# Attention scores of a hybrid encoder block: 64-row plus 128-row products become two 128-row products

## The chip, the core and the metric

The kernel runs on one core of one Trainium2 chip. The metric is device time in microseconds (us) of one execution. The core's engines work side by side and meet through semaphores: TensorE (PE, with its weight loads listed apart as PEld), VectorE (DVE), ScalarE (ACT), GpSimd (POOL), and SyncE (SP), which here issues every DMA of the program, in order.

## The reference

A block over 2048 tokens of width 1024 has two mixers side by side, an RWKV-7 group and a differential-attention group, then an output projection, a residual, and a gated feed-forward layer with a short convolution. The part that matters here is the scores of the attention group: 4 heads, each with two maps (m = 0, 1) of head dimension 64.

```python
q = _rms_norm(q.reshape(bsz, T, B_HEADS, 2, B_HEAD_DIM), q_norm_w)
k = _rms_norm(k.reshape(bsz, T, B_HEADS, 2, B_HEAD_DIM), k_norm_w)
...
s = jnp.einsum('bhmqd,bhmkd->bhmqk', q_blk, k_t).astype(jnp.float32) * scale
s = jnp.where(allowed, s + bias, -jnp.inf)
p = jax.nn.softmax(s, axis=-1)
attn = p[:, :, 0] - lam * p[:, :, 1]
```

## The kernel before

Every large product is made of parts: a float32 operand is split into a high part, `hi`, that TensorE's format holds, and the rest, `lo`; a product is then hi·hi + hi·lo + lo·hi, summed in PSUM. For most products (lines 211 to 213, 243 to 245, 960 to 962, 1003 to 1005) that is three matmuls of 128 rows.

The scores have only 64 rows (the head dimension) per map. In DRAM the queries of a head lie as three slabs of 128 rows (`g.qd`, line 1024) and the keys as two (`g.kd`). With q and k split into hi and lo, slab 0 of the queries is [lo of map 0; hi of map 0], slab 1 is [hi of map 1; lo of map 1], slab 2 is [hi of map 0; hi of map 1]. The keys' slab 0 is [hi; lo] of map 0, slab 1 is [lo; hi] of map 1. So a score tile takes two matmuls: line 719 multiplies the 64 rows of hi by hi (rows 0 to 63 of the array for map 0, 64 to 127 for map 1), and line 720 multiplies 128 rows, lo·hi + hi·lo at once.

The program runs in stages. First the input projections with the RWKV units among them (to about 1060 us of the profiled execution); then the last projections (lines 243 to 245) with the first nine steps of attention among them; then the feed-forward layer of the first half of the tokens with the rest of attention among it (to about 2390 us); at the end the feed-forward layer of the second half alone. `finish_qk` (line 264) makes the parts of queries and keys, in tiles of the tag "x" (4 buffers, shared with `vs` of `proj_v`), and stores them. `Attention.heads` steps over blocks of 256 queries and heads; each step runs `scores` of one block and head and `values` of the one before. `scores` loads the queries of the block into `qs` (line 702, two buffers), then runs over two tiles of 128 queries, two maps, and chunks of up to 512 keys; line 723 takes each score tile out of PSUM on VectorE. No table sets the order of instructions: a scheduler that simulates the engines orders the program as a whole, and each engine then keeps its order.

Of the kernel before, what the change touches and what calls it, by code (L numbers as in the profile page):

```python
# [9 lines left out]
F32 = mybir.dt.float32  # L10
F32R = mybir.dt.float32r
# [8 lines left out]
P = 128  # L20
D = 1024
KT = D // P
T = 2048
# [29 lines left out]
NH = 4  # L53
# [3 lines left out]
QB = 256  # L57
# [39 lines left out]
def split_ps(g, ps, hi, lo, scale=None):  # L97

    nc = g.nc
    if scale is None:  # L100
        nc.scalar.copy(hi, ps)
        nc.vector.tensor_sub(lo, ps, hi.bitcast(F32))
    else:
        nc.scalar.activation(hi, ps, AF.Identity, scale=scale)
        nc.vector.scalar_tensor_tensor(lo, ps, scale, hi.bitcast(F32), ALU.mult, ALU.subtract)  # L105
# [34 lines left out]
def phase1(g, ctx):  # L140
    nc, tc, a = g.nc, g.tc, g.a
    rctx = ExitStack()
    cp = rctx.enter_context(tc.tile_pool(name="p1c", bufs=1, side="right"))
    sp = rctx.enter_context(tc.tile_pool(name="p1", bufs=1, side="right"))
# [104 lines left out]
    def proj_qk(tb, hT, gi):  # L249

        qz = dn.tile([P, 4, 256], F32, name="qz", tag="qz", bufs=QZB)
        ss = dn.tile([P, 4, 4], F32, name="qss", tag="qss")
        for j, ps in token_major(tb, hT, gi):
            r1 = rsa[:, 4 * tb + j:4 * tb + j + 1]
            nc.scalar.activation(qz[:, j, :], ps, AF.Identity, scale=r1)
            sq = dn.tile([P, 256], F32, name="qsq", tag="qsq", bufs=1)
            for i in range(4):
                d = slice(i * 64, i * 64 + 64)
                nc.scalar.activation(sq[:, d], qz[:, j, d], AF.Square, accum_out=ss[:, j, i:i + 1])
        rs = dn.tile([P, 16], F32, name="qrs", tag="qrs", bufs=2)  # L260
        rsqrt(g, dn, rs, ss.rearrange("p j g -> p (j g)"), 1.0 / 64, EPS, 16, "q")
        return lambda: finish_qk(tb, gi, qz, rs)

    def finish_qk(tb, gi, qz, rs):
        is_q = gi < 9
        q3 = qz.rearrange("p j (g d) -> p (j g) d", d=64)
        nc.gpsimd.tensor_mul(q3, q3, rs.unsqueeze(2).broadcast_to((P, 16, 64)))
        for hl_ in range(2):
            h = (gi - 7) % 2 * 2 + hl_
            ps = ps_mm.tile([P, TB], F32, name="tp", tag="mm")  # L270
            for j in range(4):
                nc.tensor.transpose(ps[:, j * P:(j + 1) * P], qz[:, j, hl_ * P:(hl_ + 1) * P], ident)
            hi = dn.tile([P, TB], F32R, name="qhi", tag="x", bufs=XB)
            lo = dn.tile([P, TB], F32R, name="qlo", tag="x", bufs=XB)
            split_ps(g, ps, hi, lo, qws[:, h:h + 1] if is_q else v("kw"))
            tsl = slice(tb * TB, (tb + 1) * TB)
            dd = (g.qd if is_q else g.kd)[h].rearrange("s p t -> (s p) t")[:, tsl]
            own = dd[0:256].rearrange("(m p) t -> m p t", p=64)[0::3]
            mid = dd[64:192]
            for dst, src in ((mid, hi), (own, lo), (dd[256:384], hi)) if is_q else ((own, hi), (mid, lo)):  # L280
                nc.sync.dma_start(out=dst, in_=src.bitcast(F32))

    def proj_v(tb, hT, gi):
# [56 lines left out]
    ps = ps_mm.tile([P, 2], F32, name="lam", tag="mm")  # L340
# [312 lines left out]
class Attention:  # L653
# [44 lines left out]

    def scores(self, i, h, kg, s0s):
        g, sp, nc = self.g, self.sp, self.g.nc  # L700
        qs = sp.tile([P, 3, QB], F32R, name="qs", tag="qs", bufs=2)
        nc.sync.dma_start(out=qs.bitcast(F32), in_=g.qd[h, :, :, i * QB:(i + 1) * QB].rearrange("s p t -> p s t"))
        es = []
        for qt in range(2):
            nk = i * QB + (qt + 1) * P
            q0 = i * QB + qt * P
            nch = (nk + 511) // 512
            qsl = slice(qt * P, (qt + 1) * P)
            parts = [slice(c0, min(nk, c0 + EW)) for c0 in range(0, nk, EW)]
            ss = sp.tile([P, 2, len(parts)], F32, name="ssum", tag="ssum", bufs=2)  # L710
            e = []
            for m in range(2):
                z = [sp.tile([P, EW], F32, name=f"e{m}", tag=f"e{m}", bufs=self.eb if m == 0 else self.e1b) for _ in parts]
                mx = sp.tile([P, 4], F32, name="mx", tag="mx", bufs=2)
                for ci in range(nch):
                    n = min(512, nk - ci * 512)
                    ps = self.ps_sc.tile([P, 512], F32, name="sc", tag="sc")
                    hr = slice(0, 64) if m == 0 else slice(64, 128)
                    nc.tensor.matmul(ps[:, 0:n], qs[hr, 2, qsl], kg[ci][hr, m, 0:n], start=True, stop=False)  # L719
                    nc.tensor.matmul(ps[:, 0:n], qs[:, m, qsl], kg[ci][:, m, 0:n], start=False, stop=True)  # L720
                    b0 = (T - P) - q0 + ci * 512
                    z0 = ci * 512 % EW
                    nc.vector.tensor_tensor_reduce(z[ci * 512 // EW][:, z0:z0 + n], ps[:, 0:n], self.nd[:, b0:b0 + n], 1.0,  # L723
                                                   -3e38, ALU.add, ALU.max, mx[:, ci:ci + 1])
                nm = sp.tile([P, 1], F32, name="nm", tag="nm", bufs=2)
                nc.vector.tensor_reduce(out=nm, in_=mx[:, 0:nch], axis=AX.X, op=ALU.max)
                nc.vector.tensor_scalar(nm, nm, -SLOPES[h], None, ALU.mult)  # L727
                for pi, p in enumerate(parts):
                    zp = z[pi][:, 0:p.stop - p.start]
                    nc.scalar.activation(zp, zp, AF.Exp, bias=nm, scale=SLOPES[h], accum_out=ss[:, m, pi:pi + 1])  # L730
                e.append(z)
            st = ss[:, :, 0]
            if len(parts) == 2:
                st = sp.tile([P, 2], F32, name="ssum2", tag="ssum2", bufs=2)
                nc.vector.tensor_add(st, ss[:, :, 0], ss[:, :, 1])
            cc = sp.tile([P, 1], F32, name="cc", tag="cc", bufs=2)
            nc.vector.reciprocal(cc, st[:, 1:2])
            nc.vector.tensor_mul(cc, cc, st[:, 0:1])
            nc.vector.tensor_mul(cc, cc, g.nlam)
            for c0 in range(0, nk, 512):  # L740
                e0, e1 = [x[c0 // EW][:, c0 % EW:c0 % EW + min(512, nk - c0)] for x in e]
                nc.vector.scalar_tensor_tensor(e0, e1, cc, e0, ALU.mult, ALU.add)
            nc.vector.tensor_copy(s0s[:, qt, h:h + 1], st[:, 0:1])
            es.append(e[0])
        return es
# [268 lines left out]
def build(tc, aps, ntb=T // TB, phases=(1, 2, 3), taps=None):  # L1014
    g = Ctx()
    g.nc, g.tc, g.a, g.ntb = tc.nc, tc, aps, ntb
    taps = taps or {}
    with ExitStack() as ctx:
        dp = ctx.enter_context(tc.tile_pool(name="scratch", bufs=1, space=DRAM))

        def scratch(n, shape):
            return taps[n] if n in taps else dp.tile(shape, F32, name=n)

        g.qd = scratch("qd", [NH, 3, P, T])
        g.kd = scratch("kd", [NH, 2, P, T])
        g.vd = scratch("vd", [T, 2, B_W])
        g.yd = scratch("yd", [T, A_W])
# [104 lines left out]
```

## Time and profile before

| | |
|---|---|
| median of 3 runs | 3371.3 us (3357.81 to 3382.51) |
| profiled execution | 3374.99 us, of it 3373.2 us span |
| PE busy | 3271.8 us (97%), mean granted clock 0.962 |
| DVE, ACT, POOL busy | 61%, 45%, 20% of the span |
| DMA | 557.42 MB, mean 165 GB/s |

A busy PE is not yet PE at its peak: a matmul's duration in the trace reaches over the start of the next, since matmuls are pipelined. What a matmul takes in a stream is read from one start to the next. A clock of 1.00 in a stretch is the full 2.4 GHz, and 0.5 the lower level, 1.2 GHz.

### The profile page before, as it was taken

Reading aid. Unit: us, or ns where it says so; the run is one execution under the profiler, and the core shown is the slowest. Engines: PE = TensorE matmul, PEld = TensorE weight load, DVE = VectorE, ACT = ScalarE, POOL = GpSimd, SP = SyncE. Lnnn points to the kernel's source line nnn. Section 1 sums busy time; section 2 is a strip of 40 time slices with the busy share of each in tenths; the row PEclk is TensorE's granted clock in tenths of the full one; section 3 lists DMA queues with packets and bytes.
Section 4 is the critical chain, followed back from the end, with each engine's and each line's share of the span. In section 5 each row is a group of like instructions: output and inputs, shape, how many; then the busy total and the mean of one; then the engine's idle time right before and its main releaser. Section 6 shows DMA issues by size and latency. Waiting matters only on the chain.

```text
span 3373.2 us, 54070 instructions
## 1 busy us (share of the span) xinstructions
PE 3271.8 (97%) x19314; PEld 2687.4 (80%) x19314; DVE 2073.9 (61%) x5939; ACT 1524.8 (45%) x3391; POOL 659.9 (20%) x501
## 2 busy tenths in 40 slices
PE   8999999999999899899999999999999999999999
PEld 6777778878888788788777777777888888888887
DVE  4888868788863555677667676666643444444444
ACT  5666555555654564444444454444433322222221
POOL 4112122341322012254443101011110000000010
PEclk9999989888999899899999999999999999999999
DMA  8765544344464767455655645554574323222322
GB/s 296 252 200 176 166 144 132 108 131 145 138 193 155 251 210 256 129 199 178 208 176 195 229 153 171 176 188 155 190 281 168 100 88 113 93 83 96 104 94 94
DMA packets 391453, 557.42 MB, mean 165 GB/s; under 512 B 81040, under 2 KB 204176, under 8 KB 391056
## 3 DMA queue, kind: packets, MB, share of 16 engines
q1 hardware_dynamic: 391184, 553.96, 50.9%
q8 instruction: 153, 2.51, 0.3%
q14 instruction: 116, 0.95, 0.1%
HBM read 436.39 MB, written 117.44 MB: 164 GB/s over the span
## 4 chain that ended last, share of the span: by engine, by line
PE 85%; DMA 7%; DVE 5%; ACT 1%; issue 1%; SPq 0%; POOL 0%; ACTq 0%; DVEq 0%; POOLq 0%
PE up L962 10%; PE up L960 10%; PE up L961 10%; PE dn L1003 5%; PE dn L1004 5%; PE dn L1005 5%; PE sc L720 3%; PE sc L719 3%; PE mm L243 2%; PE mm L212 2%; PE mm L211 2%; PE mm L213 2%; PE mm L244 2%; PE mm L245 2%; PE y L569 2%; PE y L567 2%
## 5 line engine op out<-in xcount | busy, mean ns | idle before, releaser
L961 PE MATMUL up<-hT,fwhi 128*128 128x512 f32 (+1 forms) x1536 | 580.1, 379 | 0.0
L960 PE MATMUL up<-hT,fwhi 128*128 128x512 f32 (+1 forms) x1536 | 573.9, 377 | 0.9 <-DVE halo L969 0.9
L962 PE MATMUL up<-hT,fwlo 128*128 128x512 f32 (+1 forms) x1536 | 569.5, 377 | 4.5 <-DMA fwlo<-lo_w_ffn_up 4.5
L967 DVE SCALAR_TENSOR_TENSOR yy<-up,vec,yy 128x511 f32<-128x511 f32 x352 | 262.1, 745 | 349.3 <-ACT yy L964 349.1
L1006 DVE TENSOR_TENSOR acc<-dn,acc 128x512 f32<-128x512 f32 x352 | 236.7, 688 | 188.0 <-PE dn L1005 187.3
L962 PEld LDWEIGHTS up<-hT,fwlo 128*128 128x128 f32 x1536 | 291.3, 190 | 59.1 <-DMA fwlo<-lo_w_ffn_up 7.0
L961 PEld LDWEIGHTS up<-hT,fwhi 128*128 128x128 f32 x1536 | 291.2, 190 | 51.4
L960 PEld LDWEIGHTS up<-hT,fwhi 128*128 128x128 f32 x1536 | 290.0, 190 | 52.3 <-DVE halo L969 1.2
L723 DVE CUSTOM_DVE_ANT_0 e<-sc,nd 128x512 f32<-128x512 f32 (+3 forms) x320 | 191.4, 608 | 202.5 <-PE sc L720 159.8
L990 POOL TENSOR_TENSOR gl<-yy,gh 128x512 fp32r<-128x512 f32 (+1 forms) x64 | 105.8, 1654 | 1015.7 <-ACT gh L989 844.0
L117 ACT CAST fwhi<-fwraw 128x1024 fp32r<-128x1024 f32 x164 | 172.1, 1049 | 284.1 <-PE up L961 189.2
L1004 PE MATMUL dn<-dlo,gh 128*128 128x512 f32 x704 | 275.6, 392 | 1.0 <-DMA dlo<-lo_w_ffn_down 1.0
L964 ACT ACTIVATE yy<-up,vec 128x512 f32<-128x512 f32 x176 | 136.4, 776 | 305.6 <-PE up L962 305.3
L1003 PE MATMUL dn<-dhi,gh 128*128 128x512 f32 x704 | 273.7, 397 | 0.2 <-ACT dhi L117 0.2
L1005 PE MATMUL dn<-dhi,gl 128*128 128x512 f32 x704 | 261.0, 392 | 0.0
L243 PE MATMUL mm<-whi,hh 128*128 128x256 f32 x768 | 239.7, 314 | 13.7 <-DVE vs L105 8.6
L244 PE MATMUL mm<-wlo,hh 128*128 128x256 f32 x768 | 234.9, 307 | 1.5 <-DMA wlo<-lo_w_in_b 1.5
L245 PE MATMUL mm<-whi,hl 128*128 128x256 f32 x768 | 230.4, 305 | 0.0
L730 ACT ACTIVATE e<-e,nm 128x1024 f32<-128x1024 f32 (+4 forms) x192 | 171.6, 896 | 72.1 <-DVE nm L727 69.3
L211 PE MATMUL mm<-hh,whi 128*128 128x512 f32 x448 | 187.4, 420 | 10.0 <-ACT hh L201 6.8
L117 ACT CAST whi<-wraw 128x512 fp32r<-128x512 f32 x208 | 127.7, 618 | 144.2 <-PE mm L212 61.9
L212 PE MATMUL mm<-hl,whi 128*128 128x512 f32 x448 | 187.5, 418 | 0.5 <-DVE hl L202 0.5
(278 smaller groups left out, 7406.3 us busy)
## 6 DMA issues: line engine op xcount, KB each, us to landing
fwraw<-in_w_ffn_up_dram SPq DMA_DIRECT2D x132, 512.0 KB
fwlo<-lo_w_ffn_up SPq DMA_DIRECT2D x88, 512.0 KB
draw<-in_w_ffn_down_dram SPq DMA_DIRECT2D x132, 256.0 KB
vg<-vd SPq DMA_DIRECT2D x128, 256.0 KB
wraw<-in_w_in_a_dram SPq DMA_DIRECT2D x112, 256.0 KB
wraw<-in_w_in_b_dram SPq DMA_DIRECT2D x96, 256.0 KB
lo_w_ffn_up<-fwlo SPq DMA_DIRECT2D x44, 512.0 KB
dlo<-lo_w_ffn_down SPq DMA_DIRECT2D x88, 256.0 KB
```

What stands on the lines that cost most here:

```text
L117: nc.scalar.copy(hi, raw)
L212: nc.tensor.matmul(ps, whi[k], hl[k], start=False, stop=False)
L243: nc.tensor.matmul(ps, hh[k][:, ts_], whi[k], start=k == 0, stop=False)
L244: nc.tensor.matmul(ps, hh[k][:, ts_], wlo[k], start=False, stop=False)
L245: nc.tensor.matmul(ps, hl[k][:, ts_], whi[k], start=False, stop=k == KT - 1)
L960: nc.tensor.matmul(ps[:, q], wh[:, k % 4, cs], xh, start=k == 0, stop=False)
L961: nc.tensor.matmul(ps[:, q], wh[:, k % 4, cs], xl, start=False, stop=False)
L962: nc.tensor.matmul(ps[:, q], wl[:, k % 4, cs], xh, start=False, stop=k == KT - 1)
L967: nc.vector.scalar_tensor_tensor(yn[:, d:], ps[:, 0:512 - d], w, yn[:, d:], ALU.mult, ALU.add)
L1003: nc.tensor.matmul(ps, gh_[:, tsl], dh_, start=gi == 0, stop=False)
L1004: nc.tensor.matmul(ps, gh_[:, tsl], dl_, start=False, stop=False)
L1005: nc.tensor.matmul(ps, gl_[:, tsl], dh_, start=False, stop=gi == FG - 1)
```

## The change

The queries are kept as two slabs, slab 0 hi of both maps and slab 1 lo of both maps, each stored once: two stores of a head and 512 tokens instead of three. `scores` allocates one tile per map with two slabs, [hi; hi] and [lo; lo]: each is loaded by two DMAs, the same 64 rows of DRAM into the upper and into the lower half of the rows. That is four DMAs of 128 KB for a block and head instead of one of 384 KB. The tiles are two thirds as large, with three buffers instead of two. The two matmuls of a score tile now both have 128 rows: hi·(hi + lo) and lo·(hi + lo); the sum also takes in lo·lo, which was left out before.

```diff
@@ finish_qk
-            dd = (g.qd if is_q else g.kd)[h].rearrange("s p t -> (s p) t")[:, tsl]
-            own = dd[0:256].rearrange("(m p) t -> m p t", p=64)[0::3]
-            mid = dd[64:192]
-            for dst, src in ((mid, hi), (own, lo), (dd[256:384], hi)) if is_q else ((own, hi), (mid, lo)):
+            if is_q:
+                pieces = ((g.qd[h, 0, :, tsl], hi), (g.qd[h, 1, :, tsl], lo))
+            else:
+                dd = g.kd[h].rearrange("s p t -> (s p) t")[:, tsl]
+                pieces = ((dd.rearrange("(m p) t -> m p t", p=64)[0::3], hi), (dd[64:192], lo))
+            for dst, src in pieces:
                 nc.sync.dma_start(out=dst, in_=src.bitcast(F32))
@@ scores
-        qs = sp.tile([P, 3, QB], F32R, name="qs", tag="qs", bufs=2)
-        nc.sync.dma_start(out=qs.bitcast(F32), in_=g.qd[h, :, :, i * QB:(i + 1) * QB].rearrange("s p t -> p s t"))
+        qs = []
+        for m in range(2):
+            q2 = sp.tile([P, 2, QB], F32R, name="qs", tag="qs", bufs=3)
+            src = g.qd[h, :, m * 64:m * 64 + 64, i * QB:(i + 1) * QB].rearrange("s p t -> p s t")
+            for hf in range(2):
+                nc.sync.dma_start(out=q2[hf * 64:hf * 64 + 64].bitcast(F32), in_=src)
+            qs.append(q2)
...
-                    hr = slice(0, 64) if m == 0 else slice(64, 128)
-                    nc.tensor.matmul(ps[:, 0:n], qs[hr, 2, qsl], kg[ci][hr, m, 0:n], start=True, stop=False)
-                    nc.tensor.matmul(ps[:, 0:n], qs[:, m, qsl], kg[ci][:, m, 0:n], start=False, stop=True)
+                    nc.tensor.matmul(ps[:, 0:n], qs[m][:, 0, qsl], kg[ci][:, m, 0:n], start=True, stop=False)
+                    nc.tensor.matmul(ps[:, 0:n], qs[m][:, 1, qsl], kg[ci][:, m, 0:n], start=False, stop=True)
@@ build
-        g.qd = scratch("qd", [NH, 3, P, T])
+        g.qd = scratch("qd", [NH, 2, P, T])
```

The order of the program also moves. In the rows below a row is line, operation, what is written, what is read, and the size; the number behind a name tells apart the tiles that were made under that name.

The first place is TensorE in a late step of attention, among the feed-forward layer's matmuls. Before:

```order
L771 MATMUL at_22599<-ident_83,e0_21920 128x128
L719 MATMUL sc_22713<-kg_22699,qs_22707 128x512
L720 MATMUL sc_22713<-kg_22699,qs_22707 128x512
L771 MATMUL at_22599<-ident_83,e0_21980 128x128 x2
L961 MATMUL up_25723<-hT10_24419,fwhi_25718 128x512
L962 MATMUL up_25723<-hT00_24418,fwlo_25719 128x512
L719 MATMUL sc_22717<-kg_22701,qs_22707 128x512
L720 MATMUL sc_22717<-kg_22701,qs_22707 128x512
```

The same place now, where lines 725, 726, 777, 967 and 968 are the former 719, 720, 771, 961 and 962:

```order
L777 MATMUL at_22695<-ident_83,e0_22012 128x128
L725 MATMUL sc_22813<-kg_22795,qs_22803 128x512
L726 MATMUL sc_22813<-kg_22795,qs_22803 128x512
L777 MATMUL at_22695<-ident_83,e0_22072 128x128 x2
L967 MATMUL up_25835<-hT10_24527,fwhi_25830 128x512
L968 MATMUL up_25835<-hT00_24526,fwlo_25831 128x512
L725 MATMUL sc_22817<-kg_22797,qs_22803 128x512
L726 MATMUL sc_22817<-kg_22797,qs_22803 128x512
```

Here nothing moved: pairs of score products stand between the same matmuls as before.

The second place is SyncE's queue where attention begins; `kg` are keys, `vg` values, `qs` queries. Before:

```order
L694 DMA kg_12745<-kd_58 128x2x512
L702 DMA qs_12749<-qd_57 128x3x256
L702 DMA qs_12994<-qd_57 128x3x256
L757 DMA vg_13050<-vd_59 128x2x128 x2
L694 DMA kg_13263<-kd_58 128x2x512
L757 DMA vg_13321<-vd_59 128x4x128 x2
```

Now, with line 708 for the former 702:

```order
L708 DMA qs_12741<-qd_57 64x2x256 x2
L708 DMA qs_12744<-qd_57 64x2x256 x2
L708 DMA qs_12990<-qd_57 64x2x256 x2
L763 DMA vg_13050<-vd_59 128x2x128 x2
L696 DMA kg_13263<-kd_58 128x2x512
L763 DMA vg_13325<-vd_59 128x4x128 x2
L696 DMA kg_13802<-kd_58 128x2x512
L696 DMA kg_14343<-kd_58 128x2x512
L290 DMA vd_59<-vs_13709 256x1x256
L290 DMA vd_59<-vs_13719 256x1x256
L290 DMA vd_59<-vs_13765 256x1x256
L708 DMA qs_12993<-qd_57 64x2x256 x2
```

Before, the queries of the first two steps (12749, 12994) were both loaded at once. Now the first step has two tiles (12741, 12744), the second step's map 0 (12990) takes the third buffer, and its map 1 (12993) follows with eight rows between, where the first step gives a buffer back.

The third place is TensorE in the second of these steps. Before:

```order
L720 MATMUL sc_12791<-kg_12745,qs_12749 128x256
L719 MATMUL sc_12999<-kg_12745,qs_12994 128x384
L720 MATMUL sc_12999<-kg_12745,qs_12994 128x384
L719 MATMUL sc_13009<-kg_12745,qs_12994 128x384
L720 MATMUL sc_13009<-kg_12745,qs_12994 128x384
L719 MATMUL sc_13026<-kg_12745,qs_12994 128x512
```

Now, with line 813 for the former 807:

```order
L813 MATMUL ott_13072<-ident_83,ot_13070 128x128 x2
L243 MATMUL mm_13932<-whi_13909,hh0_12525 128x256
L244 MATMUL mm_13932<-wlo_13910,hh0_12525 128x256
L245 MATMUL mm_13932<-whi_13909,hl0_12533 128x256
L243 MATMUL mm_13932<-whi_13909,hh1_12526 128x256
L244 MATMUL mm_13932<-wlo_13910,hh1_12526 128x256
L245 MATMUL mm_13932<-whi_13909,hl1_12534 128x256
L243 MATMUL mm_13932<-whi_13915,hh2_12527 128x256
L725 MATMUL sc_13009<-kg_12737,qs_12993 128x384
L726 MATMUL sc_13009<-kg_12737,qs_12993 128x384
L725 MATMUL sc_13026<-kg_12737,qs_12990 128x512
L726 MATMUL sc_13026<-kg_12737,qs_12990 128x512
```

Before, the second step's score products followed one on another. Now `values` of the first step (its last product is `ott`) and seven projection matmuls stand ahead of its map 1.

## Rows read from the trace of the kernel before

**Rows 1.** The page: busy time of the engines, with share and instructions.
```profile
PE 3271.8 (97%) x19314; PEld 2687.4 (80%) x19314; DVE 2073.9 (61%) x5939; ACT 1524.8 (45%) x3391; POOL 659.9 (20%) x501
```

**Rows 2.** Busy time by stretch: PE, PEld, DVE, ACT, POOL; PEclk, DMA share, GB/s.
```profile
1060.00:1300.00 240.00, 216.36 (x1348) 181.47 (x1347) 131.70 (x577) 134.57 (x438) 28.68 (x20) 0.90 0.71 232
1300.00:2400.00 1100.00, 1084.12 (x5476) 854.02 (x5476) 727.13 (x1882) 506.90 (x889) 290.78 (x181) 0.99 0.56 183
2400.00:3373.00 973.00, 954.75 (x4783) 804.06 (x4781) 429.51 (x930) 278.79 (x370) 64.37 (x34) 1.00 0.36 123
```

**Rows 3.** Groups by shape, 1060 to 2400 us: count, busy, mean ns, idle before.
```profile
L719 PE MATMUL sc<-kg,qs 64*128 64x512 f32 x224 | 112.8, 503 | 0.6 <-DVE mx L723 0.6
L719 PE MATMUL sc<-kg,qs 64*128 64x384 f32 x32 | 14.2, 445 | 0.0
L719 PE MATMUL sc<-kg,qs 64*128 64x256 f32 x32 | 12.4, 387 | 0.0
L719 PE MATMUL sc<-kg,qs 64*128 64x128 f32 x32 | 10.5, 327 | 1.3 <-DMA kg<-kd 1.1 <-DMA qs<-qd 0.2
```

**Rows 4.** PE in order of time near 2105 us: start, us, what.
```profile
2104.14 0.40 PE L960 MATMUL up<-hT,fwhi 128*128 128x512 f32 x1
2104.37 0.40 PE L961 MATMUL up<-hT,fwhi 128*128 128x512 f32 x1
2104.70 0.49 PE L719 MATMUL sc<-kg,qs 64*128 64x512 f32 x1
2105.12 0.50 PE L720 MATMUL sc<-kg,qs 128*128 128x512 f32 x1
2105.45 0.39 PE L962 MATMUL up<-hT,fwlo 128*128 128x512 f32 x1
2105.68 0.39 PE L960 MATMUL up<-hT,fwhi 128*128 128x512 f32 x1
```

**Rows 5.** PEld, the weight loads, in the same stretch.
```profile
2104.14 0.19 PEld L961 LDWEIGHTS up<-hT,fwhi 128*128 128x128 f32 x1
2104.70 0.18 PEld L719 LDWEIGHTS sc<-kg,qs 64*128 64x128 f32 x1 [0.37 <-issue]
2105.12 0.19 PEld L720 LDWEIGHTS sc<-kg,qs 128*128 128x128 f32 x1 [0.24 <-issue]
```

**Rows 6.** PE in order of time near 1769 us, a chunk of 256 keys.
```profile
1768.95 0.39 PE L961 MATMUL up<-hT,fwhi 128*128 128x512 f32 x1
1769.27 0.38 PE L719 MATMUL sc<-kg,qs 64*128 64x256 f32 x1
1769.58 0.39 PE L720 MATMUL sc<-kg,qs 128*128 128x256 f32 x1
1769.81 0.28 PE L795 MATMUL po<-ah,vg 128*128 128x256 f32 x1
```

**Rows 7.** Line 719 by stretch: us, PE busy, PEld busy, PEclk, DMA share, GB/s.
```profile
1060.00:1300.00 240.00, 32.41 (x72) 13.73 (x72) 0.90 0.71 232
```

**Rows 8.** Instructions on `qd`: ns of one issue (min/median/max), first and last us.
```profile
L702 SPq DMA_DIRECT2D qs<-qd x32: 359/377/3956, 1085.7 to 2242.7; - x32
L281 SPq DMA_DIRECT2D qd<-qlo x16: 491/524/747, 718.3 to 1263.4; - x16
```

**Rows 9.** The chain that ended last, 1060 to 1500 us: start, us, what.
```profile
1098.69 10.52 DMA qd<-qlo
...
1172.54 3.30 DMA wlo<-lo_w_in_b
```

**Rows 10.** Waits of PE, 1060 to 1300 us: us in total, times, longest.
```profile
PE mm L243 <- DVE vs L105: 8.6, 4, 3.6
PE sc L719 <- DMA qs<-qd: 0.2, 1, 0.2
```

**Rows 11.** Waits of PE, 1300 to 2400 us.
```profile
PE up L900 <- DMA fwlo<-lo_w_out: 2.2, 2, 1.8
```

**Rows 12.** Waits of the DMA queue on SP, 1300 to 2400 us.
```profile
SPq L757 <- PE po L802: 203.7, 47, 15.2
```

## The prediction

> **What bounds the kernel now.** I read the page first, then the busy time by stretch, then the score products by shape, then TensorE's rows one by one. The page shows TensorE busy for 97% of the span, and every other engine far from it [rows 1]. By stretch it is the same where attention runs: from 1300 to 2400 us TensorE is busy for 1084 of 1100 us at a DMA share of 0.56, while from 1060 to 1300 us it is idle for 24 of 240 us, at a granted clock of 0.90 and a DMA share of 0.71 [rows 2]. So from 1300 us on, time that the score products give back is time of the program; before that only a part may be.
>
> The score products are 320 pairs: 224 with 512 keys and 32 each with 384, 256 and 128 [rows 3]. A busy time doesn't say what a pair costs, since a matmul's duration reaches over the next one's start; the starts do. Near 2105 us two neighbours of 512 columns start 0.23 us apart, from 2104.14 to 2104.37. Then line 719 starts 0.33 us after its forerunner, line 720 0.42 us after that, and the next matmul 0.33 us after line 720, whereupon 0.23 us is back [rows 4]. Three steps take 1.08 us in place of 0.69 us: the pair costs 0.39 us more than three ordinary steps. The weight loads say why. An ordinary load starts with the matmul ahead of it, so it is hidden; the loads of lines 719 and 720 start together with their own matmuls, after 0.37 and 0.24 us in which the load path stood still and waited for nothing that the profile shows ("issue") [rows 5]. With 256 keys the steps are 0.32, 0.31 and 0.23 us, in sum 0.86; the ordinary ones are 0.23 and, at half the columns, twice an estimated 0.12, in sum 0.47 [rows 6]. The excess is 0.39 us again: it does not hang on the columns. I read it as the price of changing between 128 and 64 rows and back.
>
> The Trainium skill (TensorEngine Tiling (Array Packing), Key Properties) says that a change of tiling mode drains the engine; this trace agrees, with 0.39 us for a change and back.
>
> **The change, part by part.**
>
> *Products.* 320 products of 64 rows become products of 128 rows with the same columns, between the same neighbours (the first of the places shown). All steps around them are then of the kind that takes 0.23 us for 512 columns. 320 x 0.39 = 125 us off TensorE. For the 64 products with 384 or 128 keys I have no row and take the 0.39 that 512 and 256 share. Lower end of the saving: none, if the gap is not from the rows (a rival); upper end 125, and somewhat more at half clock, where everything takes longer.
>
> *What of it reaches the end.* 72 of the 320 pairs lie in 1060 to 1300 us [rows 7], worth 28 us, where TensorE is idle for 10% [rows 2] and waits for VectorE and others [rows 10]. A faster TensorE there partly waits earlier. Between losing nothing and losing all 28 I take a third, 9 us, since TensorE is idle a tenth of that stretch and not half. After 1300 us PE's longest wait is 2.2 us in total [rows 11]; I take all of the remaining 97 us.
>
> *Loads of queries.* Four DMAs in place of one: 96 more issues of 0.377 us [rows 8] are 36 us of SP, beside SP's waits for buffers, of which one line alone has 203.7 us in this stage [rows 12] with next to nothing of it on TensorE. If that cover went, all 36 us could show; I take none. The bytes read rise by 32 x 128 KB = 4.2 MB, and the bytes written fall by 16 x 256 KB = 4.2 MB.
>
> *Buffers.* Before, two whole steps fit; now one and a half. From the second step on, map 1 of a step can only load once map 0 of the step before has had its last product, and each such load sits on SP's queue ahead of what follows. Late in the program the steps are long and this is early enough. In the first nine steps, among the projections, a step is short and TensorE may wait. A load of 256 KB took 3.30 us there [rows 9]. Below, nothing: all 32 loads of before cost TensorE 0.2 us [rows 10]. Above, each of the 15 tiles of those nine steps after the first three late by one such load, 50 us. I take 5 us, near the lower end, because the queue's order asks for each piece some products ahead, and `values` of the step before stands between (third place).
>
> *Stores.* One of three stores of each query tile goes. In the chain a store of `lo` took 10.52 us, and what came after it had to wait for its buffer [rows 9]; four waits of the projections on `vs`, 8.6 us, hang on such buffers [rows 10]. A third of that is 3 us. Ends: 0 and 8.6.
>
> *Other engines.* VectorE and ScalarE do the same work on the same tiles; VectorE, at 727 of 1100 us [rows 2], has room for a TensorE that is a tenth faster. POOL too.
>
> Sum: 3375.0 - 125 + 9 + 5 - 3 = 3261 us against the profiled execution (3374.99 us). That lies 3.7 us above the median of the three runs, so I say **3257 us**.
>
> **Rivals.**
>
> *Late queries.* The shallower buffers cost their upper end and the early stretch keeps its own pace: 3371 - 125 + 28 + 50 = 3324 us. For it: the thin first steps, a DMA share of 0.71. Against: 0.2 us of waits on queries so far [rows 10].
>
> *The change does not do what it says.* If the gaps belonged to opening or closing a score tile in PSUM and not to the rows, nothing would go: 3371 us. Against: the largest gap, 0.42 us, lies inside a tile, between its two products [rows 4], just where 64 rows become 128.
>
> *Weight loads no longer hidden.* A product of 128 rows uses the rows of its forerunner. If its load could not start early for that, each of the three steps would be as long as the one after line 720, 0.33 us: 0.99 in place of 1.08, a gain of 0.09 x 320 = 29 us, 3342 us. Against: the feed-forward layer's 128-row loads start with the matmul ahead and its steps are 0.23 us [rows 4, 5]. The Trainium skill (TensorE: Matmul & The Clock Gate, Part 3) has this rule, that a load overlaps a running matmul only where the row group differs; the trace does not bear it out.
>
> *A blocked queue: slower.* SP issues in order. In the feed-forward stage a load of queries that waits for its buffer holds back the weights behind it. The 23 steps after the first nine load 46 tiles there. Loads of values that wait for TensorE stand for 203.7/47 = 4.3 us each [rows 12]. If the queries' loads waited as long, and all of it came through to TensorE, 46 x 4.3 = 198 us would be added: 3371 - 125 + 198 = 3444 us. It decides from 125/46 = 2.7 us a load. Against: the loads of values wait that long today and weights cost TensorE 2.2 us [rows 11]; fetching ahead absorbs it.
>
> **How the numbers follow.** Forecast 0.76, late queries 0.11, no effect 0.04, loads not hidden 0.03, blocked queue 0.03; 0.03 for a gain above the range, if the moved order in the early stretch also saves idle time. The range: below, the whole 125 and the stores' 8.6, and half the 25 us that the three runs lie apart for what a moved order may do, 3225 us; above, most of the way to the late queries, 3310 us. A measurement of this kernel tells about 1% (34 us) from no change. Faster by more: the forecast, the gain above it and the late queries, 0.90; within 1%: no effect and loads not hidden, 0.07; slower: 0.03.
>
> **What would show it.** Right: steps of 0.23 us around both score products with 512 keys; their weight loads starting with the matmul ahead, without "issue" gaps; some 97 us less from 1300 us to the end of attention. Late queries: TensorE waiting for `qs` in the first nine steps. Blocked queue: SP waiting at the loads of `qs` and TensorE waiting for weights. The prediction is wrong if the score products keep gaps of 0.1 us or more, or if they close and TensorE's idle time grows by more than 50 us.

## The result, and the profile after

The changed kernel takes 3271.31 us (3270.93 to 3290.73); the kernel before, beside it, 3364.56 us. The ratio is 0.9724 [0.969, 0.9758]: 93 us are gone, where 114 were forecast. The time lies inside the range, 14 us above the forecast of 3257. The profiled execution took 3270.93 us, of it 3269.2 us span, at a mean granted clock of 0.972 (before 3374.99, 3373.2 and 0.962).

The page's line of busy times, which answers to [rows 1]:

```profile
PE 3136.8 (96%) x19314; PEld 2657.6 (81%) x19314; DVE 2085.0 (64%) x5939; ACT 1524.9 (47%) x3391; POOL 661.0 (20%) x501
```

TensorE lost 135 us of busy time, the span only 104. So its idle time grew, from 101 to 132 us. The bytes did as forecast: HBM read went from 436.39 to 440.59 MB, and written from 117.44 to 113.25 MB.

TensorE in order of time at a score pair (start, duration, what), as in [rows 4]:

```profile
2015.31 0.40 PE L966 MATMUL up<-hT,fwhi 128*128 128x512 f32 x1
2015.54 0.39 PE L967 MATMUL up<-hT,fwhi 128*128 128x512 f32 x1
2015.77 0.39 PE L725 MATMUL sc<-kg,qs 128*128 128x512 f32 x1
2016.00 0.40 PE L726 MATMUL sc<-kg,qs 128*128 128x512 f32 x1
2016.23 0.40 PE L968 MATMUL up<-hT,fwlo 128*128 128x512 f32 x1
```

And the weight loads of the same stretch, as in [rows 5]:

```profile
2015.54 0.19 PEld L725 LDWEIGHTS sc<-kg,qs 128*128 128x128 f32 x1
2015.77 0.19 PEld L726 LDWEIGHTS sc<-kg,qs 128*128 128x128 f32 x1
2016.00 0.19 PEld L968 LDWEIGHTS up<-hT,fwlo 128*128 128x128 f32 x1
```

All steps are now 0.23 us, and each load starts with the matmul ahead of it: line 725's load at 2015.54, with line 967's matmul. The steps of 0.33, 0.42 and 0.33 us and the "issue" pauses are gone. The Trainium skill (TensorE: Matmul & The Clock Gate, Part 3) has a sentence that a load overlaps a running matmul only where the row group differs, and beside it the case of a load into a background weight buffer. Here all of these matmuls use all 128 rows, and their loads of 0.19 us lie wholly beside the matmul ahead; the trace disagrees with that sentence, while the other case would allow what it shows.

Busy time by stretch (us, PE, PEld, DVE, ACT, POOL, PEclk, DMA share, GB/s), as in [rows 2]:

```profile
1060.00:1300.00 240.00, 208.69 (x1505) 194.06 (x1506) 136.71 (x581) 134.21 (x394) 43.56 (x26) 0.94 0.83 261
1300.00:2400.00 1100.00, 1063.23 (x5674) 900.97 (x5674) 780.49 (x1983) 540.15 (x941) 287.02 (x184) 0.99 0.61 201
2400.00:3269.00 869.00, 848.34 (x4245) 715.99 (x4243) 366.82 (x784) 230.88 (x296) 48.53 (x21) 1.00 0.32 106
```

Idle time of TensorE went from 24 to 31 us in the first stretch and from 16 to 37 in the second. Its waits there (us in total, times, longest), 1060 to 1300 us, as in [rows 10]:

```profile
PE mm L244 <- DMA wlo<-lo_w_in_b: 6.9, 7, 3.6
PE at L777 <- DVE e L748: 3.0, 3, 1.5
PE sc L725 <- DMA qs<-qd: 2.8, 4, 1.2
PE mm L243 <- DVE vs L105: 1.3, 3, 0.9
```

From 1300 to 2400 us, as in [rows 11]:

```profile
PE tp L930 <- DVE xq L925: 6.5, 3, 4.5
PE po L807 <- DVE al L102: 5.5, 4, 3.1
PE po L807 <- POOL al L787: 3.7, 3, 2.2
PE po L801 <- ACT ah L785: 3.7, 6, 0.7
PE up L968 <- DMA fwlo<-lo_w_ffn_up: 3.5, 6, 1.0
PE up L906 <- DMA fwlo<-lo_w_out: 3.0, 4, 1.8
PE sc L725 <- DMA kg<-kd: 2.0, 2, 1.7
```

No wait is large, and there are many kinds. Most concern chains between TensorE's own products: a result goes through VectorE, ScalarE or POOL and comes back as an operand. The whole view adds up to 36 us, where that of before adds up to 15.5.

The issues of the queries (ns of one, min/median/max), as in [rows 8]:

```profile
L708 SPq DMA_DIRECT2D qs<-qd x128: 573/597/1566, 1067.0 to 2198.0; - x128
```

One issue takes 0.597 us and not 0.377, so the four DMAs of a step keep SP busy for 128 x 0.597 = 76 us in all, in place of 12.

### The profile page after: what moved, and what is told of

The parts are those of the page before. It is cut to its first block, busy times and chain, and to the rows that moved or that the text cites. A ratio compares the mean times of both kernels' runs of the same rounds, so it can differ in the third digit from the quotient of the medians.

```text
span 3269.2 us, 54217 instructions
## 1 busy us (share of the span) xinstructions
PE 3136.8 (96%) x19314; PEld 2657.6 (81%) x19314; DVE 2085.0 (64%) x5939; ACT 1524.9 (47%) x3391; POOL 661.0 (20%) x501
## 3 DMA queue, kind: packets, MB, share of 16 engines
HBM read 440.59 MB, written 113.25 MB: 169 GB/s over the span
## 4 chain that ended last, share of the span: by engine, by line
PE 80%; DMA 9%; DVE 8%; ACT 1%; issue 1%; SPq 1%; POOL 0%; DVEq 0%; ACTq 0%; POOLq 0%
PE up L968 9%; PE up L966 9%; PE up L967 9%; PE dn L1010 5%; PE dn L1009 5%; PE dn L1011 5%; PE mm L213 3%; PE mm L211 3%; PE mm L212 3%; PE mm L243 2%; PE y L571 2%; PE y L569 2%; PE mm L244 2%; PE mm L245 2%; PE up L906 2%; DMA fwlo<-lo_w_out 2%
## 5 line engine op out<-in xcount | busy, mean ns | idle before, releaser
L243 PE MATMUL mm<-whi,hh 128*128 128x256 f32 x768 | 232.7, 304 | 11.9 <-DVE qlo L105 5.4
L244 PE MATMUL mm<-wlo,hh 128*128 128x256 f32 x768 | 227.2, 297 | 7.7 <-DMA wlo<-lo_w_in_b 7.5
L213 PE MATMUL mm<-hh,wlo 128*128 128x512 f32 x448 | 187.2, 419 | 2.1 <-POOL wlo L119 2.1
```

What stands on the lines that cost most here:

```text
L213: nc.tensor.matmul(ps, wlo[k], hh[k], start=False, stop=k == KT - 1)
L243: nc.tensor.matmul(ps, hh[k][:, ts_], whi[k], start=k == 0, stop=False)
L244: nc.tensor.matmul(ps, hh[k][:, ts_], wlo[k], start=False, stop=False)
```

## Experiments

Each ratio is to the kernel before, with its 95% interval.

**row64: the loads of the change, the products of before.**

```diff
             for hf in range(2):
-                nc.sync.dma_start(out=q2[hf * 64:hf * 64 + 64].bitcast(F32), in_=src)
+                s_ = src if hf == m else src[:, 0:1].broadcast_to((64, 2, QB))
+                nc.sync.dma_start(out=q2[hf * 64:hf * 64 + 64].bitcast(F32), in_=s_)
...
+                    hr = slice(m * 64, m * 64 + 64)
-                    nc.tensor.matmul(ps[:, 0:n], qs[m][:, 0, qsl], kg[ci][:, m, 0:n], start=True, stop=False)
+                    nc.tensor.matmul(ps[:, 0:n], qs[m][hr, 0, qsl], kg[ci][hr, m, 0:n], start=True, stop=False)
                     nc.tensor.matmul(ps[:, 0:n], qs[m][:, 1, qsl], kg[ci][:, m, 0:n], start=False, stop=True)
```

> The changed kernel with its stores, its loads (four DMAs of 128 KB a step) and its three buffers, but the two products of before: 64 rows for hi by hi, then 128 rows for the two cross terms. Theory A, the gain is the change of row count at 0.39 us a pair, and the 46 us of TensorE waits that the changed kernel has more than the kernel before come from its faster pace: the time goes back to that of before, ratio 1.00 (0.99 to 1.01), steps of 0.33, 0.42 and 0.33 us return, and TensorE's idle time falls back from 122 to about 90 us. Theory B, those waits come from the shallower buffers and the extra DMAs: ratio 1.01 to 1.02, with idle time that stays at 120 us or more. Theory C, the gain came from the stores and loads: ratio stays at 0.97.

It took 3364.04 us, ratio 0.9998 [0.9973, 1.0023]. The stores, the four DMAs (two of them read the hi slab twice, at the same size), the three buffers and the order are those of the change: by the two traces, 5 of TensorE's 19,314 matmuls stand elsewhere, on SP, DVE and ACT nothing. Together they cost nothing that the runs can tell. So the products alone make the difference: 0.9998 - 0.9724 = 0.0274 of 3365 us, 92 us, and with the two intervals added in square 78 to 106. Of 320 x 0.39 = 125 us about three quarters reach the end. TensorE in order of time there:

```profile
2034.90 0.28 PE L970 MATMUL up<-hT,fwlo 128*128 128x256 f32 x1
2035.11 0.49 PE L727 MATMUL sc<-kg,qs 64*128 64x512 f32 x1
2035.53 0.50 PE L728 MATMUL sc<-kg,qs 128*128 128x512 f32 x1
2035.87 0.28 PE L968 MATMUL up<-hT,fwhi 128*128 128x256 f32 x1
```

The longer steps are back: 0.21, 0.42 and 0.34 us, where 0.12, 0.23 and 0.23 would be ordinary, in sum 0.39 more.

As the order is the same, the two traces can be laid side by side, cut at the same instructions: first score product, first output projection, last score product. First row64, then the change:

```profile
1085.40:1266.80 181.40, 163.98 (x1022) 135.41 (x1021) 112.08 (x496) 111.85 (x356) 19.61 (x14) 0.93 0.82 250
1266.80:2370.50 1103.70, 1080.46 (x5460) 848.44 (x5461) 727.50 (x1887) 507.06 (x887) 291.09 (x180) 0.99 0.57 184
```

```profile
1075.10:1249.10 174.00, 146.45 (x1020) 133.86 (x1020) 111.65 (x497) 111.05 (x355) 19.64 (x14) 0.92 0.83 260
1249.10:2277.10 1028.00, 991.85 (x5460) 849.41 (x5461) 730.77 (x1886) 504.15 (x887) 291.07 (x179) 0.99 0.61 198
```

The same 1020 matmuls of the early piece, 66 score pairs among them, take 7 us less, of 66 x 0.39 = 26. The same 5460 of the late piece, with 254 pairs, take 76 us less, of 99. TensorE's idle time grows by 10 us in each of the two (17.4 to 27.6) and by 13 (23.2 to 36.2). In sum 83 of 125 us arrive.

Taken start by start, the 42 us that are missing fall into two parts. Of the 320 pairs, 314 stand alike in both traces. Around a pair, from the start of the product ahead of it to the start of the one behind it, the change takes 15.4 us less in the early piece and 90.5 in the late one: 106 in all, where 314 x 0.39 would be 122. In the median of the 283 pairs with no idle time by them it is 0.39 us with 512, 384 and 256 columns, and 0.34 with 128. All other steps together take 23 us more than in row64 (8 early, 15 late), 18 of them at steps where TensorE sat idle.

What TensorE waits for in the late piece can be set side by side too. Waits on results that go through VectorE, ScalarE and POOL and come back grow from 16 to 26 us, those on weights in the feed-forward and output layers from 4 to 7, and those on keys stay at 2.

**both64: both products on the same 64 rows.**

```diff
-                    nc.tensor.matmul(ps[:, 0:n], qs[m][:, 0, qsl], kg[ci][:, m, 0:n], start=True, stop=False)
-                    nc.tensor.matmul(ps[:, 0:n], qs[m][:, 1, qsl], kg[ci][:, m, 0:n], start=False, stop=True)
+                    hr = slice(m * 64, m * 64 + 64)
+                    nc.tensor.matmul(ps[:, 0:n], qs[m][hr, 0, qsl], kg[ci][hr, m, 0:n], start=True, stop=False)
+                    nc.tensor.matmul(ps[:, 0:n], qs[m][hr, 1, qsl], kg[ci][hr, m, 0:n], start=False, stop=True)
```

> The changed kernel with both products of a pair on the same 64 rows; the cross term hi of the queries by lo of the keys is left out, so this is a measurement only. If the price is the change of row count (128 to 64 and back, twice a pair as before), a pair again costs 0.39 us over three ordinary steps, and the time is that of the kernel before: ratio 1.00 (0.99 to 1.01). If each product of 64 rows has its own price, two of them cost 0.78 us a pair and the ratio is about 1.03 to 1.04. If neither costs, 0.97.

Each pair leaves out hi of the queries times lo of the keys, so this is a measurement only. It took 3373.2 us, ratio 1.0028 [1.0002, 1.0054]. TensorE in order of time:

```profile
2041.99 0.28 PE L968 MATMUL up<-hT,fwhi 128*128 128x256 f32 x1
2042.20 0.49 PE L726 MATMUL sc<-kg,qs 64*128 64x512 f32 x1
2042.54 0.39 PE L727 MATMUL sc<-kg,qs 64*128 64x512 f32 x1
2042.86 0.38 PE L969 MATMUL up<-hT,fwlo 128*128 128x256 f32 x1
2043.08 0.28 PE L967 MATMUL up<-hT,fwhi 128*128 128x256 f32 x1
```

The four steps are 0.21, 0.34, 0.32 and 0.22 us; ordinary are 0.12, 0.23, 0.23 and 0.12. The excess is 0.09, 0.11, 0.09 and 0.10, in sum 0.39 again, though there are now two products of 64 rows. Two thin products cost what one does, so the price belongs to the change of the number of rows, about 0.20 us each way, and spreads over the steps on both sides of it.

**swap: the two stores of the queries in the other order.**

```diff
-                pieces = ((g.qd[h, 0, :, tsl], hi), (g.qd[h, 1, :, tsl], lo))
+                pieces = ((g.qd[h, 1, :, tsl], lo), (g.qd[h, 0, :, tsl], hi))
```

> The changed kernel with the two stores of a query tile in the other order, lo ahead of hi. Nothing else differs, but the scheduler orders the rest of the program anew. If a moved order alone is worth little, the ratio to before is that of the changed kernel, 0.972 (0.968 to 0.976), 3262 to 3280 us. If the moved order is what took back some 25 us of the expected gain, this one lands somewhere else, by 10 us or more.

Ratio 0.973 [0.9701, 0.976]. I had meant it to move the order of the whole program a little. It didn't: by the trace even the two stores are still issued hi first, lo second, and the 2097 DMAs of SP and all instructions of VectorE and ScalarE stand as in the change. So it says only that the same order gives the same time, and nothing of what an order is worth.

**qtile: the same four DMAs, cut by query tile and not by map.**

```diff
-        for m in range(2):
-            q2 = sp.tile([P, 2, QB], F32R, name="qs", tag="qs", bufs=3)
-            src = g.qd[h, :, m * 64:m * 64 + 64, i * QB:(i + 1) * QB].rearrange("s p t -> p s t")
+        for qt in range(2):
+            q2 = sp.tile([P, 4, P], F32R, name="qs", tag="qs", bufs=3)
+            t0 = i * QB + qt * P
+            src = g.qd[h, :, :, t0:t0 + P].rearrange("s (m p) t -> p (s m) t", p=64)
...
-                    nc.tensor.matmul(ps[:, 0:n], qs[m][:, 0, qsl], kg[ci][:, m, 0:n], start=True, stop=False)
-                    nc.tensor.matmul(ps[:, 0:n], qs[m][:, 1, qsl], kg[ci][:, m, 0:n], start=False, stop=True)
+                    nc.tensor.matmul(ps[:, 0:n], qs[qt][:, m], kg[ci][:, m, 0:n], start=True, stop=False)
+                    nc.tensor.matmul(ps[:, 0:n], qs[qt][:, 2 + m], kg[ci][:, m, 0:n], start=False, stop=True)
```

> The changed kernel with the queries' tiles cut by query tile (128 queries, both maps) and not by map: the same three buffers of 2 KB a partition, the same four DMAs of 128 KB a step, but pieces of 512 B in place of 1 KB. The second tile of a step is then needed only after all of the first tile's products, and its buffer comes free half a step earlier. If late queries took back part of the gain (theory B), 20 us or more come back: ratio 0.960 to 0.967. If the waits come from the faster pace (theory A), the ratio stays within 0.3% of the changed kernel's 0.972.

Ratio 0.9801 [0.9762, 0.984], 0.8% slower than the change, which neither theory had foreseen. That the queries' buffers come free earlier buys nothing that shows: from 1060 to 2400 us TensorE waits 2.0 us for `qs`, in the change 2.8. What made it slower is not settled: the pieces are half as long, the order moved too, and its largest waits of 1300 to 2400 us are not on queries:

```profile
PE po L808 <- DVE al L102: 8.9, 5, 3.1
PE up L907 <- DMA fwlo<-lo_w_out: 8.7, 4, 3.7
```

**ygroup: the lesson carried to the RWKV products.** There 512 products of 128 rows and 512 of 64 rows, 64 columns wide, alternate, in the trace mostly two by two; eight of one kind are put ahead of eight of the other.

```diff
                     nc.tensor.matmul(y4[yq, i, hd, :], xm[c][:, i, hd, C:2 * C], sh[c][:, i, hd, :],
-                                     start=True, stop=False)
+                                     start=hd == 0 and i == 0, stop=False)
+            for hd in range(2):
+                for i in range(GP):
                     nc.tensor.matmul(y4[yq, i, hd, :], rb[ub, i, hd, :], su[c][ub, i, hd, :],
-                                     start=False, stop=True)
+                                     start=False, stop=hd == 1 and i == GP - 1)
```

> The changed kernel with the same lesson applied to the RWKV units: the sixteen small products of a chunk's y, which alternate between 128 rows and 64 rows, are issued as eight of 128 rows and then eight of 64 (only the first opens the accumulation). In the changed kernel's trace 425 such changes stand there, each about 0.09 us longer than its columns ask, 39 us in sum; 64 changes, some 6 us, are left. If a change of row count has its price there too and TensorE is the bound in that stage (busy for 95% of it), 20 to 33 us go: ratio to before 0.962 to 0.967. If the units' chain through VectorE sets that stage's pace, the ratio stays at 0.972.

Ratio 0.9739 [0.9703, 0.9776]: no gain over the change. Yet the busy time went (busy, mean ns, idle before), here of the change and then of ygroup:

```profile
L569 PE MATMUL y<-sh,xm 128*64 128x64 f32 x512 | 85.0, 249 | 5.0 <-DVE yt L594 5.0
L571 PE MATMUL y<-su,rb 64*64 64x64 f32 x512 | 84.2, 245 | 0.0
```

```profile
L569 PE MATMUL y<-sh,xm 128*64 128x64 f32 x512 | 43.0, 237 | 1.4 <-DVE sh L563 1.4
L573 PE MATMUL y<-su,rb 64*64 64x64 f32 x512 | 42.1, 226 | 0.0
```

84 us of busy time are off these lines. By the starts, which count, the price of a change of rows is there too. First the changed kernel, then ygroup:

```profile
809.34 0.33 PE L569 MATMUL y<-sh,xm 128*64 128x64 f32 x2
809.60 0.33 PE L571 MATMUL y<-su,rb 64*64 64x64 f32 x2
```

```profile
818.28 1.14 PE L573 MATMUL y<-su,rb 64*64 64x64 f32 x16
819.35 0.68 PE L569 MATMUL y<-sh,xm 128*64 128x64 f32 x8
```

Two products of one kind take 0.26 us from start to start of the pairs, and sixteen in a row 1.07 us, with steps of 0.058. So a change of rows costs 0.14 us. The whole program has 810 changes of rows in the change's trace and 402 in this one's, which makes about 57 us. The first score product comes at 1011 us in place of 1075. But the stage around it doesn't turn this into time. From 700 to 1075 us, first the change, then ygroup:

```profile
700.00:1075.00 375.00, 359.69 (x3364) 317.23 (x3363) 263.61 (x880) 212.64 (x664) 99.91 (x93) 0.95 0.53 157
```

```profile
700.00:1075.00 375.00, 331.30 (x3145) 300.84 (x3144) 253.79 (x914) 203.57 (x657) 91.82 (x84) 0.88 0.55 161
```

TensorE is idle for 44 us there in place of 15, and the granted clock of the stretch is 0.88 in place of 0.95. The whole program's busy time fell by 32 us only, not by 84. TensorE is idle for 181 us (a span of 3285.4 less 3104.4 busy) in place of 132. The mean granted clock is 0.958 in place of 0.972, so the time at the lower level is 2 x (1 - 0.958) x 3285 = 276 us in place of 2 x (1 - 0.972) x 3269 = 183. So the time taken off came back as idle time and as matmuls at the lower clock. Which of the two brought on the other, and what the stage then waits for, no run separates.

**lora128: two more kinds of 64-row products made 128 rows, with zeros in the other half.**

```diff
+    zwd = cp.tile([P, SB], F32, name="zwd")
+    nc.gpsimd.memset(zwd[64:128], 0.0)
+    zwa = cp.tile([P, SB], F32, name="zwa")
+    nc.gpsimd.memset(zwa[0:64], 0.0)
...
-            nc.tensor.matmul(lpw[:, p], wda[0:64, p * P:(p + 1) * P], zw[0:64], start=True, stop=True)
+            nc.tensor.matmul(lpw[:, p], wda[:, p * P:(p + 1) * P], zwd, start=True, stop=True)
...
-            nc.tensor.matmul(lpa[:, p], wda[64:128, p * P:(p + 1) * P], zw[64:128], start=True, stop=True)
+            nc.tensor.matmul(lpa[:, p], wda[:, p * P:(p + 1) * P], zwa, start=True, stop=True)
```

> The changed kernel with the two 64-row products of each RWKV unit that make its decay and its gate done as 128-row products, by two copies of the small input with zeros in the other half. In the changed kernel's trace the changes around them are worth 9 us. With a price per change of row count: 5 to 9 us less than the changed kernel, ratio 0.969 to 0.971; else 0.972 or, through the second small DMA of a unit, a little more.

Ratio 0.9837 [0.9785, 0.9889], slower than the change. The products' busy time gained nothing; here of the change, then of lora128:

```profile
L393 PE MATMUL lpw<-zw,wda 64*128 64x128 f32 x128 | 20.1, 302 | 0.2 <-DVE rq_x_k L87 0.2
L399 PE MATMUL lpa<-zw,wda 64*128 64x128 f32 x128 | 19.8, 289 | 1.8 <-ACT thw L396 1.8
```

```profile
L397 PE MATMUL lpw<-zwd,wda 128*128 128x128 f32 x128 | 20.9, 312 | 1.5 <-DVE rq_x_k L87 1.5
L403 PE MATMUL lpa<-zwa,wda 128*128 128x128 f32 x128 | 22.2, 310 | 3.6 <-ACT thw L400 3.6
```

There were hardly any changes of rows to save: the traces have 810 in the change and 796 here. The two input tiles have one buffer each in place of one tile with two, and the order moved; from 700 to 1300 us TensorE waits 15.3 us for `qs` and 15.0 for `wlo`, in the change 2.8 and 7.5. Which of the two made it slower wasn't separated.

**ygroup_lora: both of these edits together.**

> Both of these on the changed kernel: if they add, ratio 0.959 to 0.965, 3230 to 3248 us; if the RWKV stage has another bound, 0.970 to 0.973.

Ratio 0.9687 [0.965, 0.9724]. One edit alone is no gain, the other alone a loss of 1%, and together there is no loss left: the interval lies clear below that of lora128 and overlaps that of the change. The effects of such edits don't add.

**nohalo: VectorE relieved.** The line of the short convolution that adds the two columns at a tile's edge is left out: 352 instructions, half of the 704 that were counted beforehand.

```diff
-                            nc.vector.scalar_tensor_tensor(yn[:, 0:d], halo[:, fb, 2 - d:], w, yn[:, 0:d], ALU.mult, ALU.add)
```

> The changed kernel without the two small VectorE operations per feed-forward tile that add the convolution's carried columns (left out, so a measurement only): 704 instructions, 119 us of VectorE's busy time alone and more with their start, 72 us of it in the 1100 us from 1300 us on. If what the changed kernel gave back in that stage are waits on VectorE at TensorE's faster pace, 10 to 25 us come back: ratio 0.964 to 0.969. If they are waits on weights from DRAM, nothing: 0.972.

Ratio 0.9701 [0.9654, 0.9748], not to be told from the change. The stretch where the score products lie:

```profile
1300.00:2400.00 1100.00, 1061.24 (x5660) 899.68 (x5659) 722.66 (x1804) 539.58 (x939) 287.17 (x182) 0.99 0.62 202
```

VectorE is busy for 58 us less than in the change, and TensorE idle for 39 us as against 37. The two ratios allow anything from 12 us lost to 27 gained, so the times alone don't exclude the 10 to 25 us that were expected; that the idle time stayed speaks against them. The line removed lies outside the chains that TensorE waits for most (on `xq`, `al`, `ah`), so this says something of VectorE's load and nothing of those chains.

**nokeep: a fifth of the DMA traffic taken away.** The low parts of the feed-forward and output weights are made on POOL at every use, not stored and loaded.

```diff
-        return load_split(self.g, self.g.fw, tag, self.g.a[name][at], shape, bufs, self.g.kept[name][at], self.t00 == 0)
+        return load_split(self.g, self.g.fw, tag, self.g.a[name][at], shape, bufs, None, True)
```

> The changed kernel with the low parts of the feed-forward and output weights made on GpSimd at every pass and neither stored nor loaded: 200 loads and 96 stores of weights, some 115 of 557 MB of DMA traffic less, for 200 more subtractions on GpSimd, some 390 us of it, which is busy for 20% now. If what the changed kernel gave back are waits that DMA traffic makes longer, TensorE's idle time from 1060 us to the end falls by 20 us or more and the ratio to before is 0.960 to 0.967. If they are waits along the chain transpose, split, product through ScalarE and VectorE, or the scheduler's fixed order, the ratio stays at 0.97; if GpSimd becomes late, it is above 0.98.

Ratio 0.9722 [0.9679, 0.9765], the change's own. The same stretch:

```profile
1300.00:2400.00 1100.00, 1050.82 (x5562) 893.96 (x5562) 804.37 (x1957) 525.18 (x924) 464.07 (x272) 0.98 0.41 128
```

The DMA share fell from 0.61 to 0.41, and TensorE is idle for 49 us in place of 37. POOL and VectorE have more to do, which may hide a small gain; a large one from less traffic is not there.

**Three looks at the order.** All of them change one constant of the program's order. yl_heads12 (`HEADS1 = 12`) and yl_ha0 (`HA1 = 0`) start from ygroup_lora, ha0 (`HA1 = 0`) from the change. `HA1` raises the priority of the first attention steps, and `HEADS1` is their number.

```diff
-HP, HA1, HA = 3000, 400, 0
+HP, HA1, HA = 3000, 0, 0
...
-HEADS1 = 9
+HEADS1 = 12
```

> The kernel with both changes in the RWKV units (ratio 0.969 so far) with 12 in place of 9 attention steps among the last projections. There the units end 35 to 64 us earlier, attention starts earlier and TensorE then waits for its first loads. If more steps of attention beside projections fill that stretch, ratio 0.960 to 0.966; if the loads of that stretch are what is short, 0.970 or more.

> The same kernel, with 9 steps, but without the raised priority of those attention steps over the projections. If TensorE's waits at the start of attention come from score products that are ordered ahead of projections although their loads are still under way, 5 to 20 us go: ratio 0.963 to 0.967. If not, 0.969 or, with attention pushed later, above it.

> The changed kernel with only the raised priority of the first nine attention steps taken away; the RWKV units are as in the changed kernel. If the order of those steps is what gave back part of the change's gain, 10 to 25 us come back: ratio 0.963 to 0.969, and TensorE's idle time falls below 122 us. If the 0.961 of the kernel with both unit changes and this priority came mostly from the units, the ratio stays at 0.972 (0.969 to 0.976).

yl_heads12 has 0.968 [0.9652, 0.9709], the same as ygroup_lora. **yl_ha0 has 0.9612 [0.9584, 0.9639], 3241.26 us: the fastest of all, faster than both kernels.** ha0 has 0.9739 [0.97, 0.9778], no gain, though by the trace another product stands at 3944 of TensorE's 19,314 places. So the same constant is worth about 25 us beside the two RWKV edits and nothing without them. From 1300 to 2400 us, ygroup_lora first, then yl_ha0:

```profile
1300.00:2400.00 1100.00, 1048.41 (x5495) 887.39 (x5494) 757.55 (x1925) 522.81 (x912) 281.67 (x180) 0.98 0.60 197
```

```profile
1300.00:2400.00 1100.00, 1065.27 (x5652) 902.91 (x5650) 764.73 (x1933) 529.72 (x919) 286.12 (x182) 0.98 0.61 201
```

TensorE's idle time in this stretch is 52 us in the one and 35 in the other; over the whole program it is 180 and 157. Why the order fits there and not in the change stays open.

## Why the prediction was right, and where it was short

*The price of a pair: right.* The steps after are 0.23 us; row64 brings the longer steps back and with them the whole time of before; both64 shows that the price is that of a change of rows and not of a thin product. That the 64 pairs with 384 or 128 keys cost as much was taken without a row; it was right for 384 (0.39 us) and nearly so for 128 (0.34). The Trainium skill (TensorEngine Tiling (Array Packing), Key Properties) says that a change of tiling mode drains the engine and gives no figure. The runs here agree that a change has a price, about 0.20 us among these products; the draining itself no trace shows.

*What of it reaches the end: mis-sized.* The step that fell short is "I take all of the remaining 97 us". In the late piece 76 of 99 us arrived, by the two traces with one order. Against the kernel before itself the same piece is 60 us shorter (1088 to 1028), with six pairs more in it, where the sign that I named was some 97. I had taken TensorE's wait of 2.2 us on weights [rows 11] and its busy share for proof that nothing else was near. But 2.2 us was not TensorE's longest wait after 1300 us. Two chains of its own products stood above it already:

```profile
PE tp L924 <- DVE xq L919: 3.1, 3, 2.3
PE po L795 <- ACT ah L779: 3.0, 3, 1.5
```

And a full engine says only that little else is late at its present pace. The chains that run through VectorE, ScalarE and POOL and back keep their own length, and with a faster TensorE they end last more often. The lists of waits at one order bear this out: of the 13 us by which TensorE's idle time grew in the late piece, 10 are waits on such results and 3 on weights. Why they grew is still argued: a run in which one such chain alone is made shorter was not made. What the runs show besides is that it is not the loads, buffers and stores by themselves (row64). Large effects of VectorE's load (nohalo) and of the traffic (nokeep) are not there, small ones aren't excluded.

*The early stretch: right in kind, short in size.* I let 19 of 28 us through; 7 of 26 came. TensorE's idle time there grew by 10 us at the same granted clock (0.93 and 0.92).

*Head of the program: not foreseen, and mostly not of the change.* By the profiles the 104 us between the two executions are 23 ahead of any score product, 28 in the early piece (which has six pairs fewer now) and 60 in the late one, less 7 that the rest took longer. The 23 were forecast nowhere: the first score product came at 1097.7 us before and at 1075.1 after. Of these, 14.5 us lie in a part where TensorE starts the same 4862 matmuls, all but four in the same order, up to 741.3 and 726.8 us, at a granted clock of 0.92 and 0.94. In row64, with the order of the change, the first score product came at 1085.4, in both64 at 1076.5. I count most of this as scatter between executions and not as gain; what the moved stores add to it isn't separated. The forecast went from an execution of 3374.99 us by the three runs' median of 3371.3. From the 3364.56 beside the result the same sum gives 3251 us, so that 7 of the 21 us by which the gain fell short were made good by luck.

*Queries and their buffers: right.* TensorE waits 2.8 us for `qs` where I said 5, between 0 and 50. SP waits 52.8 us at line 708 for the products of the step before, and issues for 76 us instead of the 48 that I had counted, and next to nothing waits for it: row64 has all of this and is not slower.

*Stores: right in size, and gone elsewhere.* The waits on `vs` went from 8.6 to 1.3 us, but those on `wlo` came from 1.5 to 6.9, at a DMA share of 0.83 in place of 0.71. The 3 us that I booked did not show.

*Sum.* Forecast 125 - 9 - 5 + 3 = 114 us. By the traces with one order 125 - 19 (early) - 23 (late) = 83 us, by the medians 92 to 93 us. TensorE's idle time grew by 31 us, inside the 50 that would have spoken against the prediction.

*Rivals.* "No effect" falls by the result and row64, "weight loads no longer hidden" by the loads that start with the matmul ahead, "blocked queue" by 6.5 us of waits on `fwlo`. "Late queries" forecast 3324 us, and its sign, TensorE waiting for `qs`, came to 2.8 us.

## What to carry to other kernels

Read the cost of a small product from the starts of its neighbours, not from its busy time: a product of 64 rows among products of 128 rows cost 0.39 us more than one of 128 rows, whether it had 512, 384 or 256 columns, and two in a row cost no more than one. Fill the rows, or put the thin products together. Then don't book all of such a saving, even on a full engine: here two thirds to three quarters arrived in all, and 7 of 26 us in the early piece, where TensorE already waited; other kernels were not measured. List every chain that TensorE waits for, however short, for these ended last more often afterwards. And try the order of the program anew after such an edit, since effects of 1% moved with it and did not add.

## What the runs showed of the hardware beyond that

A DMA of 128 KB onto 64 rows took 0.597 us to issue on SP, one of 384 KB onto 128 rows 0.377 us. Less data was dearer to issue. The form of the source matters little: 0.597 us again in row64, where half of these DMAs read one slab twice, and 0.607 in qtile, with pieces of half the length. Two plain loads onto 64 rows at the start of the program (lines 303 and 304) took 0.582 and 0.490 us. That points to the rows, but no run changes them alone.

The alternating RWKV products, 64 columns wide, cost 0.14 us for each change of rows. The score products cost 0.17 with 128 columns and about 0.20 with 256 and more. So the price doesn't hang on the columns from 256 up, and is smaller for shorter products.
